# A decoder trunk on one core: x and memory read depth-first, the first block of columns computed before the rows' scales are known

## The chip, the cores and the metric

The kernel runs on one core of a Trainium2 chip. Its engines work side by side: TensorE multiplies matrices (PE in the rows; PEld is its loading of the stationary operand), VectorE (DVE) and ScalarE (ACT) work on tiles, GpSimd (POOL) does some of the same more slowly, and SyncE (SP) issues most of the transfers. The metric is the device time of one execution in microseconds (us), as a median of several runs.

## What is computed

One layer of a hybrid decoder, all in float32, with x of 1024 rows by 2048 and a memory of 256 rows by 2048:

```
h   = rmsnorm(x, norm_mix)                    # each row by 1/rms, each column by its gain
y   = h @ w_in                                # 2048 x 7184: q, k, v and gates of three mixers
mix = [stick_breaking(8 heads), gated_linear(4 heads), spatial_gating(4 groups)]
x   = x + (rmsnorm_per_head(mix) * silu(gates)) @ w_out
m   = rmsnorm(mem, norm_mem)
x   = x + cross_attention(rmsnorm(x, norm_xattn), m, w_xq, w_xkv, w_xo)
out = rmsnorm(x, final_norm)
```

The change concerns the first line, the memory's norm, and the columns of `y` that are computed first: `SB_V`, 1024 columns of v for the stick-breaking heads, and `GL_V`, 512 columns of v for the gated linear attention.

## The kernel before

Every large product is made from operands that are split in two (`hi`, a rounded copy, and `lo`, what is left), so that three matmuls stand for one: `mm3` issues hi by lo, hi by hi, lo by hi. A weight piece of 128 rows by up to 512 columns is loaded by `raw_weights` (three buffers `wr`), ScalarE casts it to `wh` and VectorE subtracts to get `wl` (three buffers each; `split_to`, L143 and L144). The left operand of all the first products is `hT`: the normed x, transposed, 2048 deep on the partitions (16 pieces `k` of 128) by 1024 rows in two halves of 512.

The order of the work is that of the program as far as the operands allow: a scheduler sorts each engine's queue ahead of time by program order and readiness. Where `pinned` is set, TensorE's instructions keep the order in which they are written. Memory pools are opened and closed by name, and a pool that is opened takes the place of one that was closed.

The stages, in order:

1. The first stage (pool `xin`). Eight row tiles of x (128 rows by 2048) and then two of memory are loaded. `normed` squares a row tile on ScalarE (L340), finds 1/rms (`rstd_of`) and scales the tile on VectorE (L348, with the gain `gbc`, which is broadcast over the partitions). `turn` transposes it on TensorE in pieces of 128 by 128 (`flip`, L180) and splits the result from PSUM into `hT`. While the next row tile is made ready, the first 256 columns of `SB_V` are computed for the tile before, from eight weight pieces that stay in memory. Then the second 256 columns are computed for all rows, with the rows in two halves. Transposed memory goes through scratch in DRAM (`memt_scr`). The results of v go to scratch (`v_scr`, L311, L312, L314).
2. Six blocks of 512 columns for all 1024 rows: the second half of `SB_V`, then `gv`, `su`, `sv`, `sg`, `gg` (`natural`, pool `st0`; each result is stored to DRAM from a tile `nt`, L460 and L461).
3. Keys and values of the memory (pool `kv`): for each of 16 `k` the transposed memory is loaded (L476) and split, two weight pieces are loaded and split, and 12 matmuls of 512 columns add into four banks `pj`, which are all that there are of that kind.
4. The rest, which the change leaves as it is: the gating unit (pool `sgu`), gated linear attention, stick-breaking attention beside the projections of k and q, the output projection, attention over the memory and the last norm.

A block's matmuls are counted in steps: in the blocks whose rows are in two halves, a step is one `k` for four row tiles, 12 matmuls; its plan is `[(k, r) for r in halves for k in range(KT)]`, 32 steps.

Of the kernel before, what the change touches and what calls it, by code (L numbers as in the profile page):

```python
# [17 lines left out]
P = 128  # L18
S = 1024
D = 2048  # L20
# [21 lines left out]
def trunk(ctx, tc, x, mem, norm_mix, w_in, w_gla_gate_up, b_gla_gate, sgu_norm, w_sgu, b_sgu,  # L42
          out_norm, w_out, norm_xattn, norm_mem, w_xq, w_xkv, w_xo, final_norm, out, dbg=None):
# [3 lines left out]
    x2d, mem2d, out2d = x[0], mem[0], out[0]  # L47
    w_in3 = w_in[0].rearrange("(k p) n -> p k n", p=P)
# [22 lines left out]
    class Operand:  # L71
        """[2048, 1024] with its first axis on partitions, as two tiles that add up to it, by four k and half."""
# [15 lines left out]
    def scratch(name, shape):  # L88
# [5 lines left out]
    make_identity(nc, ident)  # L94
# [7 lines left out]
    layout = (("out", out_norm[0], 16), ("xat", norm_xattn[0], 16), ("mem", norm_mem[0], 16), ("bg", b_gla_gate[0], 2),  # L102
              ("bs", b_sgu[0], 4))
    cols_at, n_cols = {}, 0
    for nm, _, n in layout:
        cols_at[nm] = n_cols
        n_cols += n
    cols = const.tile([P, n_cols], F32, name="cols")

    def load_cols():  # L110
        """Vectors that act per partition, one column for each 128 values."""
        rows = wraw.tile([P, 512], F32, tag="wr", name="rows")
        for nm, src, n in layout:
            c = cols_at[nm]
            sp.dma_start(rows[c:c + n, :P], src if nm == "bs" else src.rearrange("(k p) -> k p", p=P))
        tp = bank("pj")
        pe.transpose(tp[:, :n_cols], rows[:n_cols, :P], ident[:n_cols, :n_cols])
        dve.tensor_copy(cols, tp[:, :n_cols])

# [8 lines left out]
    def rstd_of(ss, n, count):  # L128
        """(ss / count + eps) ** -0.5, with a Newton step after the tables."""
# [29 lines left out]
    def weights(src, width, sub=1, hl=None, raw=None, eng=None):  # L159
        """A [P, sub * width] piece of a weight, as two tiles that add up to it."""  # L160
# [34 lines left out]
    def column_block(acts, w3, c0, evac, halves=(0, 1)):  # L195
        """[n, s] tiles of the product for 128 columns, in four groups of a load and four steps."""
# [27 lines left out]
    def weave(groups, tasks):  # L224
        """Steps in order, each task before the step that its time names, loads a group ahead."""
# [91 lines left out]
    with tc.tile_pool(name="xin", bufs=2) as xin, tc.tile_pool(name="w0", bufs=1) as w0p:  # L317
# [5 lines left out]
        def load_rows(src):  # L323
            xt = xin.tile([P, D], F32, tag="xt", name="xt", bufs=3)
            for sl in pieces:
                sp.dma_start(xt[:, sl], src[:, sl])
# [892 lines left out]
```

## Time and profile before

| | |
|---|---|
| median of 3 runs | 2186.11 us |
| lowest and highest | 2184.13 and 2188.30 us |
| the profiled execution, from its first to its last instruction | 2184.6 us |
| TensorE busy | 2125.8 us, 97% |
| VectorE busy | 1020.7 us, 47% |
| ScalarE busy | 860.9 us, 39% |
| GpSimd busy | 163.5 us, 7% |
| mean memory traffic | 106 GB/s |

The profiled execution has no time of its own beside its span; the span of 2184.6 us is set beside the median. Busy is the time in which an engine had an instruction under way. Matmuls are pipelined: a row of the trace gives a matmul's time from start to modelled end, and the distance between the starts of two matmuls in a row is what one costs in a stream.

### The profile page before, as it was taken

What the parts mean: (1) busy time and instruction counts of PE and PEld (TensorE: products, weight loads), DVE (VectorE), ACT (ScalarE), POOL (GpSimd) and SP (SyncE); (2) the same over time, 40 slices, a digit from 0 to 9 for tenths busy, and PEclk for the clock granted to TensorE, in tenths of its full rate; (3) what the DMA queues carried; (4) which work ended last, traced back from release to release, by engine and by line L of the source; (5) the groups of instructions that cost most, each with busy time, mean ns of one, the idle gap of its engine ahead of it and who ended that gap; (6) DMA issues with size and microseconds to landing.
All of it is one profiled execution on the core that took longest, in us unless ns stands there. A gap on an engine that the chain in (4) does not pass through costs nothing.

```text
span 2184.6 us, 28465 instructions
## 1 busy us (share of the span) xinstructions
PE 2125.8 (97%) x10525; PEld 1767.4 (81%) x10525; DVE 1020.7 (47%) x1984; ACT 860.9 (39%) x1987; POOL 163.5 (7%) x273
## 2 busy tenths in 40 slices
PE   6999999999999999999999999999989999999997
PEld 6998888888887767878888888888877878888885
DVE  6621211111115627375377677776753121377674
ACT  6421111221215424242356565666654121356552
POOL 2110000000000110101111111111012000000001
PEclk9999999999999999999999999999999999999999
DMA  7541321331317621313222222222267231655632
GB/s 215 151 146 49 126 87 49 97 97 49 98 55 219 184 61 44 107 34 92 78 57 55 56 63 56 61 54 56 83 192 231 69 124 49 207 201 154 216 121 92
DMA packets 181847, 231.18 MB, mean 106 GB/s; under 512 B 17270, under 2 KB 106956, under 8 KB 179532
## 3 DMA queue, kind: packets, MB, share of 16 engines
q1 hardware_dynamic: 170572, 214.68, 32.1%
q0 software_dynamic: 11136, 14.69, 2.6%
q8 instruction: 83, 1.36, 0.3%
q14 instruction: 56, 0.46, 0.1%
HBM read 177.93 MB, written 51.38 MB: 105 GB/s over the span
## 4 chain that ended last, share of the span: by engine, by line
PE 44%; DVE 8%; ACT 5%; issue 4%; DMA 2%; POOL 1%; DVEq 0%; SPq 0%; POOLq 0%; ACTq 0%
PE pj L175 31%; PE z L175 6%; PE av L175 4%; PE tr L180 1%; DVE a L865 1%; DVE a L871 1%; PE tr L175 1%; ACT a L872 1%; DMA mraw<-mix 1%; ACT t L859 1%; ACT t L860 1%; DVE t L861 1%; DVE ql L663 1%; ACT t L858 1%; DVE wl L144 1%
## 5 line engine op out<-in xcount | busy, mean ns | idle before, releaser
L144 DVE TENSOR_TENSOR wl<-wr,wh 128x512 fp32r<-128x512 f32 (+1 forms) x392 | 267.6, 683 | 773.8 <-ACT wh L143 767.6
L175 PE MATMUL pj<-slot,wh 128*128 128x512 f32 x2048 | 576.9, 398 | 1.6 <-DVE qT L144 1.6
L143 ACT CAST wh<-wr 128x512 fp32r<-128x512 f32 (+1 forms) x395 | 237.6, 602 | 798.4 <-PE av L175 548.6
L175 PE MATMUL pj<-wh,slot 128*128 128x512 f32 (+1 forms) x1760 | 500.7, 370 | 0.0
L175 PEld LDWEIGHTS pj<-slot,wh 128*128 128x128 f32 x2048 | 369.7, 188 | 72.4 <-issue 2.3
L175 PEld LDWEIGHTS pj<-wh,slot 128*128 128x128 f32 x1760 | 321.5, 190 | 54.8
L175 PE MATMUL pj<-wl,slot 128*128 128x512 f32 (+1 forms) x880 | 328.9, 374 | 1.7 <-DVE wl L144 1.5
L175 PE MATMUL pj<-slot,wl 128*128 128x512 f32 x1024 | 327.9, 391 | 0.0
L175 PEld LDWEIGHTS pj<-slot,wl 128*128 128x128 f32 x1024 | 192.2, 188 | 42.7
L175 PEld LDWEIGHTS pj<-wl,slot 128*128 128x128 f32 x880 | 167.1, 190 | 30.3 <-DVE wl L144 2.3
L175 PE MATMUL z<-wh,slot 128*128 128x512 f32 x576 | 178.6, 390 | 0.7 <-DVE slot L144 0.7
L175 PEld LDWEIGHTS z<-wh,slot 128*128 128x128 f32 x576 | 108.2, 188 | 24.1 <-DVE slot L144 1.9
L175 PE MATMUL z<-wl,slot 128*128 128x512 f32 x288 | 112.5, 391 | 4.4 <-DVE xo L982 2.7
L861 DVE SCALAR_TENSOR_TENSOR t<-z,t 128x384 f32<-128x384 f32 (+2 forms) x96 | 53.4, 556 | 94.3 <-ACT t L860 94.2
L872 ACT ACTIVATE a<-a 128x384 f32<-128x384 f32 (+2 forms) x96 | 50.4, 525 | 114.5 <-DVE a L871 114.4
L175 PE MATMUL pj<-slot,oT 128*128 128x512 f32 x384 | 92.7, 396 | 0.0
L175 PE MATMUL tr<-wh,slot 128*128 128x512 f32 x288 | 88.7, 389 | 0.0
L175 PE MATMUL av<-wh,slot 128*128 128x512 f32 x288 | 88.7, 389 | 0.0
L175 PEld LDWEIGHTS pj<-slot,oT 128*128 128x128 f32 x384 | 71.0, 188 | 15.7
L175 PE MATMUL z<-kT,qT 128*128 128x512 f32 (+3 forms) x288 | 71.1, 355 | 0.0
L175 PEld LDWEIGHTS z<-wl,slot 128*128 128x128 f32 x288 | 54.0, 188 | 17.2 <-DVE xo L982 3.6
L144 DVE TENSOR_TENSOR aTl<-tr,aTh 128x512 fp32r<-128x512 f32 (+2 forms) x112 | 55.2, 493 | 19.3 <-ACT aTh L143 18.2
(252 smaller groups left out, 2684.2 us busy)
## 6 DMA issues: line engine op xcount, KB each, us to landing
wr<-in_w_in_dram SPq DMA_DIRECT2D x216, 256.0 KB, 2.8
wr<-in_w_out_dram SPq DMA_DIRECT2D x88, 256.0 KB, 2.8
xt<-in_x_dram SPq DMA_DIRECT2D x32, 256.0 KB, 4.8
wr<-in_w_xkv_dram SPq DMA_DIRECT2D x32, 256.0 KB, 3.2
v<-v_scr POOLq DMA_DIRECT2D x64, 128.0 KB, 2.8
xr<-in_x_dram SPq DMA_DIRECT2D x32, 256.0 KB, 5.1
x<-xo SPq DMA_DIRECT2D x32, 256.0 KB, 4.4
x2t<-x SPq DMA_DIRECT2D x8, 1024.0 KB, 7.2
```

The costliest lines, as they stand in the source:

```text
L143: act.copy(hi, src)
L144: eng.tensor_tensor(out=lo, in0=src, in1=f32(hi), op=ALU.subtract)
L175: i = pe.matmul(o, l, r, start=start, stop=stop)
L180: i = pe.transpose(o, i_, ident)
L663: dve.tensor_tensor(out=gl["ql"][r_, :, hh, :].rearrange("p c (b i) -> p c b i", i=h), in0=gl["q"][r_, :].rearrange("p (c b i) -> p c b i" ...
L858: act.activation(tw, z, AF.Abs)
L859: act.activation(tw, tw, AF.Exp, scale=-1.0)
L860: act.activation(tw, tw, AF.Ln, bias=1.0)
L861: dve.scalar_tensor_tensor(out=tw, in0=z, scalar=0.0, in1=tw, op0=ALU.max, op1=ALU.add)
L865: dve.tensor_tensor_scan(out=aw[:, ::-1], data0=tw[:, ::-1], data1=tw[:, ::-1], initial=init, op0=ALU.add, op1=ALU.max)
L871: dve.tensor_tensor(out=aw, in0=z, in1=aw, op=ALU.subtract)
L872: act.activation(aw, aw, AF.Exp)
```

## The change

x and the memory are also handed over transposed (`xT`, `memT`: 2048 deep by 1024 or 256), and the gains that act per partition come as columns of one small array (`cols`, `mix`). With depth on the partitions, the gain `norm_mix` is a number per partition, while 1/rms is a number per row, that is, per column of the operand, and is known only when a whole row has been squared and summed.

- Pieces of `xT` (128 by 512) arrive one at a time. `arrive` splits a piece, times its gain, into `hT` (`split_gain`: ScalarE for hi, VectorE for lo), squares it on ScalarE and adds the square to a running sum on GpSimd.
- The block `GL_V` is computed from these unscaled operands, rows in two halves: 32 steps. Its results are scaled by 1/rms as they leave the banks; those of the first half are kept and scaled later.
- Before step 26 `scales` sums the squares over the partitions on TensorE: eight products with two columns of ones, and two with a matrix of ones, which give 1/rms in every partition (`r_all`).
- From step 27 to step 58 `rescale` loads each piece of `xT` again, multiplies it by gain and 1/rms on VectorE and splits it into the same place of `hT`. The first half of `SB_V` (512 columns wide, rows in two halves) is steps 32 to 63 and uses the rescaled operand, as does all that follows.
- The memory's pieces are loaded transposed, split with their gain, and the results are scaled by the memory's 1/rms, whose squares are taken from rows of memory loaded in the same loop (at `k` = 4 and 6).
- The transposes of x and memory, the row norms, the memory's scratch and the 256-wide passes are gone. The scratch stores of v are on SyncE. The pools of the gating unit and of the memory open after the pool `st0` closes, and the identity for later transposes is made after the first two blocks.

```diff
-        def turn_x(s, kg):
-            split_to(*hT.group(kg, s), transposes(xs[s], kg))
...
-        def turn_mem(m, kg):
-            tp = transposes(xs[ST + m], kg)
...
-            pool.dma_start(memt_scr[m][4 * kg:4 * kg + 4].rearrange("k p m -> p k m"), mt)
...
-            (pool if "at" in kw or nh == 2 else sp).dma_start(v_scr[s][:, h0:h0 + nh], vt)
+            sp.dma_start(v_scr[s][:, h0:h0 + nh], vt)
...
-    sgu_open()
     kv = Stage("kv", 2)
-    kv.open()
+    halves = (range(4), range(4, 8))
 
     with tc.tile_pool(name="st0", bufs=2) as st0:
-        natural(hT, w_in3, SB_V + 512, 512, evac_v(st0, 512, 4, tag="vt"))
...
+        with tc.tile_pool(name="xin", bufs=1) as xin:
+
+            sp.dma_start(cols, cols_in[:, :n_cols])
+            mix = xin.tile([P, KT], F32, name="mix")
+            sp.dma_start(mix, cols_in[:, n_cols:n_cols + KT])
+            squares = xin.tile([P, 2, 512], F32, name="squares")
+            r_all = xin.tile([P, 2, 512], F32, name="r_all")
+            unscaled, r_row = {}, []
+
+            def staged():
+                return xin.tile([P, 512], F32, tag="xt", name="xt", bufs=6)
+
+            def piece(k, half):
+                xt = staged()
+                sp.dma_start(xt, xT3[:, k, half * 512:half * 512 + 512])
+                return xt
+
+            def arrive(k, half):
+                xt = piece(k, half)
+                split_gain(*hT.at(k, half), xt, mix[:, k:k + 1])
+                if k == 0:
+                    act.activation(squares[:, half], xt, AF.Square)
+                else:
+                    sq = xin.tile([P, 512], F32, tag="sq", name="sq", bufs=2)
+                    act.activation(sq, xt, AF.Square)
+                    pool.tensor_tensor(out=squares[:, half], in0=squares[:, half], in1=sq, op=ALU.add)
+
+            def scales():
+                b = bank("pj")
+                for s in range(ST):
+                    mm(b[:, 2 * s:2 * s + 2], squares[:, s // 4, (s % 4) * P:(s % 4) * P + P], ones_f[:, 0:2], True, True)
+                sums_ = [bank("pj"), bank("pj")]
+                for h in range(2):
+                    mm(sums_[h], ones_f, squares[:, h], True, True)
+                for h in range(2):
+                    v_, y_, t_ = staged(), staged(), staged()
+                    dve.tensor_scalar(out=v_, in0=sums_[h], scalar1=1.0 / D, scalar2=EPS, op0=ALU.mult, op1=ALU.add)
+                    act.activation(y_, v_, AF.Ln)
+                    act.activation(y_, y_, AF.Exp, scale=-0.5)
+                    dve.scalar_tensor_tensor(out=t_, in0=y_, scalar=-0.5, in1=y_, op0=ALU.mult, op1=ALU.mult)
+                    dve.tensor_tensor(out=t_, in0=t_, in1=v_, op=ALU.mult)
+                    dve.scalar_tensor_tensor(out=r_all[:, h], in0=t_, scalar=1.5, in1=y_, op0=ALU.add, op1=ALU.mult)
+                ss = xin.tile([P, ST], F32, name="ss")
+                dve.tensor_copy(ss, b[:, 0:2 * ST:2])
+                r_row.append(rstd_of(ss, ST, D))
+                for s in range(4):
+                    act.activation(unscaled[s], unscaled[s], AF.Copy, scale=r_row[0][:, s:s + 1])
+                    sp.dma_start(nat_scr["gv"][s], unscaled[s])
+
+            def rescale(k, half):
+                xt = piece(k, half)
+                dve.scalar_tensor_tensor(out=xt, in0=xt, scalar=mix[:, k:k + 1], in1=r_all[:, half], op0=ALU.mult, op1=ALU.mult)
+                split_to(*hT.at(k, half), xt)
+
+            def keep(s, b):
+                t = unscaled[s] = xin.tile([P, 512], F32, tag=f"gv{s % 4}", name=f"gv{s}")
+                if s < 4:
+                    (dve.tensor_copy if s % 2 else act.copy)(t, b)
+                else:
+                    act.activation(t, b, AF.Copy, scale=r_row[0][:, s:s + 1])
+                    sp.dma_start(nat_scr["gv"][s], t)
+
+            by_half = [(k, r) for r in halves for k in range(KT)]
+            steps_ = row_block(hT, w_in3, GL_V, 512, keep, by_half) + \
+                row_block(hT, w_in3, SB_V, 512, evac_v(st0, 0, 4, tag="vt"), by_half)
+            extra = [[] for _ in range(64)]
+            order_ = [(k, half) for half in range(2) for k in range(KT)]
+            for n, (k, half) in enumerate(order_):
+                j = k if half == 0 else (n - 16) * 4 + 3 if n < 21 else n - 5
+                extra[j].append((arrive, k, half))
+                extra[27 + n if n < 5 else 27 + n].append((rescale, k, half))
+            extra[26].append((scales,))
+            steps_[0][0]()
+            for j, (_, do) in enumerate(steps_):
+                for f, *args in extra[j]:
+                    f(*args)
+                if j + 1 < len(steps_):
+                    steps_[j + 1][0]()
+                do[0]()
+        make_identity(nc, ident)
+        natural(hT, w_in3, SB_V + 512, 512, evac_v(st0, 512, 4, tag="vt"))
...
-        for nm, c0, func in (("gv", GL_V, AF.Copy), ("su", SG_U, AF.Gelu_apprx_tanh), ("sv", SG_V, AF.Gelu_apprx_tanh),
+        for nm, c0, func in (("su", SG_U, AF.Gelu_apprx_tanh), ("sv", SG_V, AF.Gelu_apprx_tanh),
...
+    sgu_open()
+    kv.open()
...
     for k in range(KT):
         mt = kv.tile([P, 256], F32, tag="mt", name="mt")
-        for m in range(2):
-            sp.dma_start(mt[:, m * P:m * P + P], memt_scr[m][k])
+        sp.dma_start(mt, memT3[:, k, :])
...
-        split_to(hl[0], hl[1], mt)
+        split_gain(hl[0], hl[1], mt, col("mem", k))
+        if k in (4, 6):
+            for n in range(4):
+                mr = kv.tile([P, 512], F32, tag="mr", name="mr")
+                m = k // 2 - 2
+                sp.dma_start(mr, mem2d[m * P:m * P + P, n * 512:n * 512 + 512])
+                act.activation(mr, mr, AF.Square, accum_out=ss_mem[:, m, n:n + 1])
...
-        dve.tensor_copy(vt, mem_banks[m][1])
+        dve.tensor_scalar(out=vt, in0=mem_banks[m][1], scalar1=r_mem[:, m:m + 1], scalar2=None, op0=ALU.mult)
...
-        act.copy(kt, mem_banks[m][0])
+        act.activation(kt, mem_banks[m][0], AF.Copy, scale=r_mem[:, m:m + 1])
```

## Rows read from the trace of the kernel before

**Rows 1.** The page's first part: busy time, share of the span, instructions.

```profile
PE 2125.8 (97%) x10525; PEld 1767.4 (81%) x10525; DVE 1020.7 (47%) x1984; ACT 860.9 (39%) x1987; POOL 163.5 (7%) x273
```

**Rows 2.** Windows by stage: length, busy by engine, granted clock, DMA share, GB/s.

```profile
24.43:134.42 109.99, 107.02 (x889) 104.73 (x887) 66.49 (x157) 53.33 (x152) 14.03 (x22) 1.00 0.56 161
134.42:657.31 522.89, 522.68 (x2304) 432.15 (x2303) 74.85 (x115) 92.89 (x154) 2.81 (x5) 1.00 0.27 82
657.31:706.27 48.96, 47.88 (x193) 34.45 (x192) 26.02 (x45) 26.12 (x50) 0.00 (x0) 1.00 0.72 213
```

**Rows 3.** Waits of TensorE, 0 to 250 us: total, times, longest.

```profile
PE z L180 <- DVE xt L348: 13.9, 2, 9.7
```

**Rows 4.** Timeline of TensorE: start, duration, instruction, count of merged instructions.

```profile
15.39 0.41 PE L175 MATMUL pj<-wl,slot 128*128 128x256 f32 x1
...
16.03 0.41 PE L175 MATMUL pj<-wl,slot 128*128 128x256 f32 x1
...
21.09 1.09 PE L180 MATMUL z<-ident,xt 128*128 128x128 f32 x4 [4.22 <-DVE xt L348]
...
24.43 0.60 PE L180 MATMUL z<-ident,xt 128*128 128x128 f32 x4
24.79 0.36 PE L175 MATMUL pj<-w0l,slot 128*128 128x256 f32 x1
...
119.91 0.40 PE L175 MATMUL pj<-wh,slot 128*128 128x256 f32 x2
...
120.27 0.40 PE L175 MATMUL pj<-wh,slot 128*128 128x256 f32 x2
...
601.55 0.39 PE L175 MATMUL tr<-wl,slot 128*128 128x512 f32 x1
...
602.23 0.39 PE L175 MATMUL av<-wl,slot 128*128 128x512 f32 x1
```

**Rows 5.** Groups by line and form, 0 to 150 us: count, busy, mean, idle.

```profile
L180 PE MATMUL z<-ident,xt 128*128 128x128 f32 x160 | 26.6, 295 | 17.3 <-DVE xt L348 13.9 <-DVE slot L144 3.4
```

**Rows 6.** Timeline of SyncE and ScalarE at the start; issues with median landing.

```profile
0.81 1.81 SPq L326 DMA_DIRECT2D xt<-in_x_dram  x4
...
3.96 0.60 ACT L340 ACTIVATE tr<-xt 128x512 f32<-128x512 f32 x1 [1.88 <-DMA xt<-in_x_dram]
...
5.17 0.60 ACT L340 ACTIVATE av<-xt 128x512 f32<-128x512 f32 x1 [0.48 <-DMA xt<-in_x_dram]
...
xt<-in_x_dram SPq DMA_DIRECT2D x32, 256.0 KB, 4.8
```

**Rows 7.** Timelines of GpSimd and VectorE, later stages.

```profile
720.06 1.66 POOL L543 TENSOR_TENSOR y<-y,sg 128x512 f32<-128x512 f32 x1 [570.56 <-ACT wh L143]
...
720.50 1.77 DVE L144 TENSOR_TENSOR wl<-wr,wh 128x512 fp32r<-128x512 f32 x1
...
1629.60 1.29 DVE L144 TENSOR_TENSOR slot<-mraw,slot 128x512 fp32r<-128x512 f32 x2 [2.77 <-ACT slot L143]
```

**Rows 8.** Instructions of one tile or line: ns least, median, most.

```profile
L970 POOL TENSOR_TENSOR mraw<-mraw,graw x16: 1275/1292/1645, 1617.1 to 1665.3; 128x512 f32<-128x512 f32 x16
...
L524 DVE SCALAR_TENSOR_TENSOR sv<-sv,rs_r,gn x8: 744/748/1870, 495.0 to 761.4; 128x512 f32<-128x512 f32 x8
```

**Rows 9.** Timeline of TensorE: matmuls of operands that are not split.

```profile
714.55 1.06 PE L175 MATMUL z<-sv,wT 128*128 128x128 f32 x8
...
808.10 1.12 PE L175 MATMUL z<-rr,wup 32*128 32x512 f32 x2
```

**Rows 10.** The change to the memory stage: SyncE, landing times; GpSimd's groups.

```profile
658.65 0.32 SPq L461 DMA_DIRECT2D gg<-nt  x1
...
gg<-nt SPq DMA_DIRECT2D x8, 256.0 KB, 2.0
mt<-memt SPq DMA_DIRECT2D x24, 64.0 KB, 3.1
...
L579 POOL MEMSET maskf<- 128x448 f32 x1 | 0.5, 473 | 6.4 <-DMA mix<-mt 6.4
```

More of the change, by code (lines that the diff above doesn't have):

```diff
@@ L41, in trunk @@
 @with_exitstack
-def trunk(ctx, tc, x, mem, norm_mix, w_in, w_gla_gate_up, b_gla_gate, sgu_norm, w_sgu, b_sgu,
-          out_norm, w_out, norm_xattn, norm_mem, w_xq, w_xkv, w_xo, final_norm, out, dbg=None):
+def trunk(ctx, tc, x, mem, w_in, w_gla_gate_up, sgu_norm, w_sgu, w_out, w_xq, w_xkv, w_xo, final_norm,
+          xT, memT, cols_in, out, dbg=None):
     nc = tc.nc
@@ L47, in trunk @@
     x2d, mem2d, out2d = x[0], mem[0], out[0]
+    xT3 = xT.rearrange("(k p) s -> p k s", p=P)
+    memT3 = memT.rearrange("(k p) m -> p k m", p=P)
     w_in3 = w_in[0].rearrange("(k p) n -> p k n", p=P)
@@ L100, in trunk @@
     dve.memset(eps_t, EPS)
-    layout = (("out", out_norm[0], 16), ("xat", norm_xattn[0], 16), ("mem", norm_mem[0], 16), ("bg", b_gla_gate[0], 2),
-              ("bs", b_sgu[0], 4))
+    layout = (("out", 16), ("xat", 16), ("mem", 16), ("bg", 2), ("bs", 4))
     cols_at, n_cols = {}, 0
-    for nm, _, n in layout:
+    for nm, n in layout:
         cols_at[nm] = n_cols
@@ L108, in trunk @@
     cols = const.tile([P, n_cols], F32, name="cols")
[L110 to L118, printed above, removed]
     def col(nm, k):
@@ L292, in trunk @@
     nat_scr = {nm: [scratch(f"{nm}{s}", [P, 512]) for s in range(ST)] for nm in ("su", "sv", "sg", "gv", "gg")}
-    memt_scr = [scratch(f"memt{m}", [KT, P, P]) for m in range(2)]
     kt_scr = [scratch(f"kt{m}", [P, 4, P]) for m in range(2)]
@@ L307, in f @@
         def f(s, b):
-            vt = kw["at"](s) if "at" in kw else pl.tile([P, nh, 2, P], F32, name="vt", **kw)
+            vt = pl.tile([P, nh, 2, P], F32, name="vt", **kw)
             b3 = b.rearrange("p (h d) -> p h d", d=P)
-            hi = vt[:, :, 0, :]
-            act.copy(hi.bitcast(F32R), b3)
-            dve.tensor_tensor(out=vt[:, :, 1, :].bitcast(F32R), in0=b3, in1=hi, op=ALU.subtract)
+            act.copy(vt[:, :, 0, :].bitcast(F32R), b3)
+            dve.tensor_tensor(out=vt[:, :, 1, :].bitcast(F32R), in0=b3, in1=vt[:, :, 0, :], op=ALU.subtract)
@@ L482, in trunk @@
                 mm3(mem_banks[m][n], cut(hl, m * P, m * P + P), w, k == 0, k == KT - 1)
+    r_mem = kv.tile([P, 2], F32, name="r_mem", bufs=1)
+    sst_mem = small.tile([P, 2], F32, tag="ss2", name="ss2")
+    dve.tensor_reduce(out=sst_mem, in_=ss_mem, axis=AX.X, op=ALU.add)
+    dve.tensor_copy(r_mem, rstd_of(sst_mem, 2, D))
     mem_k = []
@@ L1196, in trunk @@
         dbg(locals())
-_INS = ["x", "mem", "norm_mix", "w_in", "w_gla_gate_up", "b_gla_gate", "sgu_norm", "w_sgu", "b_sgu", "out_norm",
-        "w_out", "norm_xattn", "norm_mem", "w_xq", "w_xkv", "w_xo", "final_norm"]
+_INS = ["x", "mem", "w_in", "w_gla_gate_up", "sgu_norm", "w_sgu", "w_out", "w_xq", "w_xkv", "w_xo", "final_norm"]
 def kernel(**inputs):
@@ L1208 @@
     nc = bacc.Bacc("TRN2", target_bir_lowering=False, num_devices=1)
+    laid = {name: inputs[name] for name in _INS}
+    laid["xT"], laid["memT"] = (np.asarray(inputs[nm])[0].T for nm in ("x", "mem"))
+    laid["cols"] = np.concatenate([np.asarray(inputs[nm]).reshape(-1, P) for nm in
+                                   ("out_norm", "norm_xattn", "norm_mem", "b_gla_gate", "b_sgu", "norm_mix")]).T
     arrays, args = {}, []
-    for name in _INS:
-        a = np.ascontiguousarray(inputs[name])
+    for name in laid:
+        a = np.ascontiguousarray(laid[name])
         arrays[f"in_{name}_dram"] = a
```

88 lines of the change are left out of this document (1 added, 87 removed).

## The prediction

> **What bounds the kernel now.** The page's first part comes first: TensorE is busy for 97% of the span, VectorE for under half [rows 1]. So the question is what TensorE does and where it is idle. The windows cut at the places where its work changes [rows 2] give the answer. From 134.42 to 657.31 us, six blocks of 512 columns (the second half of v, then gv, su, sv, sg, gg) run with no gap, 522.89 / 6 = 87.15 us each. Before 134.42 lies the stage that the change rewrites. After it come the memory's keys and values, 48.96 us for 192 matmuls. At the 0.227 us of a 512-wide matmul (below) those need 43.6, so 5.4 us are lost there.
>
> What the first 134.42 us hold is read from the timeline of TensorE. Three 256-wide matmuls repeat every 0.36 us (119.91 to 120.27, [rows 4]), 0.12 us each; 768 of them are 92.2 us. Four transposes take 0.36 us (24.43 to 24.79, [rows 4]), 0.09 each; the 160 of x and memory [rows 5] are 14.4 us. The rest, 134.4 - 92.2 - 14.4 = 27.8 us, is idle time and a slow clock. TensorE first waits 9.7 us for the first scaled row and once more 4.2 us for the second, 13.9 together [rows 3]. Until 24.43 us three 256-wide matmuls take 0.64 us (15.39 to 16.03, [rows 4]), 0.213 us each: 256 columns at 1.2 GHz, the lower of the two levels. After it they run at the higher.
>
> TensorE is never long idle from there to the end, so a microsecond that the first stage gives back is a microsecond of the whole, unless a wait takes its place.
>
> **The change part by part.** I follow the time at which the memory's matmuls start, 657.31 now; the work behind it is the same.
>
> *Blocks.* The 256-wide passes become one 512-wide block. Three 512-wide matmuls repeat every 0.68 us (601.55 to 602.23, [rows 4]), 0.227 each, against 2 x 0.36 = 0.72 for the same columns. Seven blocks at 87.15 are 610.0 us. The transposes, the row of 54 vectors, the per-row norms and the memory's way through DRAM are gone.
>
> *First matmul.* Two small loads, then the first weight, then the first x piece are issued on SP. An issue costs 1.81 / 4 = 0.45 us [rows 6], so the weight is issued at 1.7 and x at 2.2. The first piece now lands 3.96 - 0.81 = 3.15 us after its issue and the next 1.2 us behind it [rows 6]. That puts the weight at 4.9, x at 6.1 and, after a 0.60 us cast, the first matmul at 6.8 us (5.9 if x does not queue behind the weight, 8.5 if it lands after 4.8 us, the median for x [rows 6]).
>
> *Slow clock.* TensorE worked without a break from 21.09 to 24.43 before it ran at the higher level [rows 4]. If dense work from 6.8 us does likewise, 3.3 us pass at 0.12 / 0.213 = 0.56 of the rate: 1.5 us lost. The other bound is all of 9.70 to 24.43, 14.7 x 0.44 = 6.5 us. I take 1.5, since the new stream has no such gaps by the budgets below.
>
> *Scales on TensorE.* Eight tiny fp32 matmuls and two of 512 columns. Eight fp32 ones of 128 columns last 1.06 us, two of 512 (32 rows high) 1.12 [rows 9], both with tails that overlap what follows: together about 1.9, with 1.06 + 2 x 1.12 = 3.3 as the upper bound if full height makes the wide ones twice as slow, and 1.1 as the lower if the tiny ones cost nothing.
>
> *The arriving operand.* One step is four row tiles, 12 x 0.227 = 2.72 us. Up to step 26, 32 x pieces and 27 weights are split on ScalarE and VectorE, and GpSimd adds 30 squares. ScalarE pays 0.6 us a pass: (27 + 2 x 32) x 0.6 = 55 us of the 73.4 that 27 steps take, so it is covered. VectorE and GpSimd are not so clear. When a GpSimd add (720.06, 1.66 us) and a VectorE subtract of two SBUF operands (720.50, 1.77 us) meet, VectorE ends at 722.27, 0.55 us after the add; alone, two such subtracts take 1.29 us, 0.61 apart [rows 7]. So VectorE stands still while GpSimd adds. The old operand was split from PSUM; the new one is split from SBUF, against those adds. As one shared resource the pair needs 27 x 0.61 (weights, [rows 7]) + 32 x 0.68 (three operands; 0.748 alone [rows 8], less the 0.07 overlap of the subtracts) + 30 x 1.29 [rows 8] = 77.0 us. TensorE needs 73.4 + 1.5 in the same steps. That is a tie, 2.1 us against us. Were they independent, VectorE's 38 us would be hidden and this term nothing. If every add is held up as the one at 720.06 was (1.65), the pair needs 87.8 and TensorE waits 14.4 - 1.5 = 12.9 us. I take 3, near the tie, for the splits run ahead by three weight buffers.
>
> The Trainium skill, GPSIMD Engine Reference, section Specifications, says that GpSimd shares its SBUF interfaces with VectorE and contends with VectorE instructions that have two SBUF inputs; the trace agrees with its 1.77 us, and it speaks against this part of the change.
>
> *Rescale in place.* After the scales the chain is: two reductions read, logarithm, exponential, a Newton step (about 4.2 us for the first half, from three VectorE passes of 0.75 [rows 8] behind two ScalarE passes of 0.6 and one read of 0.7), then the x piece again (4.8 to land), and 0.75, 0.60 and 1.29 - 0.61 = 0.68 to scale and split it: 11.0 us. The first rescaled piece is wanted at step 32, six steps or 16.3 us later. It fits with 5.3 us spare, and ScalarE can split the weights of steps 27 to 31 in the gaps. After that each step wants 0.61 + 0.68 + 0.61 = 1.9 us of VectorE in 2.72. If that cover goes, step 32 is late, and everything behind it. I allow 1 us (0 to 5), and 1 us (0 to 3) for the v stores, which now stand on SP's queue between the weights and the x pieces.
>
> *DMA.* Weights and x are read twice in these 64 steps, 512 KB in 2.72 us or 193 GB/s. The memory stage now moves 213 [rows 2], so it is hidden; without that cover each step would lose the difference.
>
> *Memory stage.* One load of memory in place of two per step, but eight more loads and 4.8 us of ScalarE for its squares. Between all of the 5.4 lost us won and as many lost again, I take zero.
>
> Sum: 6.8 + 610.0 + 1.5 + 1.9 + 3 + 1 + 1 = 625.2, against 657.31: 32.1 us won. The profiled execution spans 2184.6 us and the median of the runs is 2186.11, 1.5 more. 2184.6 - 32.1 + 1.5 = 2154.0 us.
>
> **Rivals.** *A, the memory stage starts late.* The pools of the gating unit and of the memory now open after the pool of the 512-wide results closes. At a later change of pools GpSimd's first write into the new pool waited 6.4 us for the last store of the old one [rows 10]. If the memory's loads wait so, the last store (issued 658.65, 2.0 to land) ends at 660.7; two loads of the gating unit go first (0.8), then 3.1 to land and 0.8 to split [rows 10]: 665.4. TensorE idles 8.1 us and pays the slow clock's 1.5 again: 2163.6. For it: every bank of the first kind is taken by the memory's own sums, so nothing can fill the gap. Against: the memory's tiles may lie where only the first stage's were, and then load early, as now.
>
> *B, VectorE and GpSimd bind the first block.* The 12.9 us from above in place of 3: 2163.9, and up to 2168 if the scales are late by as much as they have spare.
>
> *C, slower than before: the clock stays low.* If waits between steps keep TensorE at the lower level, 512 columns cost 0.427 in place of 0.227, over the first block's 32 steps 32 x 12 x 0.2 = 77 us. It decides from 32.1 / 77 = 42% of the block, 13 steps, on; with all of it the time is 2154 + 77 = 2231, with 60% of it 2200. For it: before, the level was low through the whole start with its 4.2 us gap. Against: the granted clock was full in all three windows from 24.43 on [rows 2], and gaps by the budget are tenths of a microsecond a step.
> The Trainium skill, TensorE: Matmul & The Clock Gate, section Loop structure matters more than you think, warns of loops in which TensorE waits for a load between matmuls and then runs at the lower rate; the first 24 us agree (0.213 us for 256 columns).
>
> **How the numbers follow.** Forecast 0.58 (its own range 2146 to 2160: no stalls and a better memory stage at one end, the bounds of the smaller terms at the other), A 0.18, B 0.16, C 0.05, and 0.03 for waits that eat the gain just about. The range 2146 to 2168 leaves out C, the last case and the edges of the others, 2 in 10. Faster by over 0.2% (about the spread of the runs before, 2184.13 to 2188.30, and what a measurement can tell) 0.93, within it 0.02, slower 0.05.
>
> **What would show it.** First matmul near 6.8 us and full clock by about 11; twelve 512-wide matmuls per 2.72 us in the first block with waits on VectorE of 3 us in all (B: 13); adds of about 1.3 us with VectorE's splits stretched to 1.8 beside them; no wait of TensorE at the first rescaled piece; the memory's first matmul at about 625 us right behind the last gg matmul (A: 8 us of idle time there). The prediction is wrong if TensorE waits at the scales or at the pool change for more than a few microseconds, or if the sum of the stage before 134.42 us does not shrink to about 102 us (625.2 less six blocks).

## The result and the profile after

The changed kernel takes 2166.45 us (median of four runs, 2165.18 to 2167.51) against 2187.2 (2184.13 to 2190.08) on the same chip: a ratio of 0.9906, interval 0.9894 to 0.9918. It is faster, as forecast, by 20.7 us, where 32 were worked out. The time lies near the upper end of the range of 2146 to 2168, where rival B was put, and outside the forecast's own 2146 to 2160. The profiled execution spans 2164.6 us, 20.0 less than before.

The page's first part, which answers to [rows 1]:

```profile
PE 2108.2 (97%) x10000; PEld 1735.2 (80%) x10000; DVE 1077.2 (50%) x1978; ACT 890.6 (41%) x1975; POOL 186.3 (9%) x271
```

Windows of the changed kernel, in the columns of [rows 2]; the third is the memory stage:

```profile
6.35:49.90 43.55, 37.92 (x138) 29.17 (x139) 42.09 (x33) 33.78 (x59) 33.07 (x21) 0.92 0.69 221
49.90:100.00 50.10, 46.09 (x200) 36.95 (x199) 29.92 (x36) 21.43 (x39) 15.13 (x10) 0.97 0.42 122
640.22:691.09 50.87, 47.41 (x194) 35.02 (x193) 28.32 (x51) 28.80 (x54) 0.67 (x1) 1.00 0.79 246
```

VectorE, under half busy over the whole, is busy for 42.09 of the 43.55 us in which the operand arrives, with GpSimd at 33.07 beside it. TensorE does not fill that stretch, and its granted clock is not full. (The column of the granted clock has no record of the start, until the level first rises near 11 us; there the level is read from the distance of the matmuls.) The waits of TensorE in the first 300 us, where [rows 3] had 13.9 us:

```profile
PE pj L166 <- DVE wl L135: 9.6, 6, 2.1
PE pj L166 <- ACT slot L138: 6.3, 1, 6.3
PE z L166 <- DVE wl L135: 0.6, 1, 0.6
```

The 6.3 is the start. The other 10.2 us are waits for VectorE's split of a weight: 9.6 while the operand arrives, the last at 61.32 us, and 0.6 that ends at 187.4 us, in the second block, where the kernels without adds on GpSimd wait too (1.0 us in kernels 1 and 2 below). The timeline of TensorE shows where they fall and what follows:

```profile
6.35 0.80 PE L166 MATMUL pj<-wl,slot 128*128 128x512 f32 x1 [6.35 <-ACT slot L138]
...
11.38 0.39 PE L166 MATMUL pj<-wl,slot 128*128 128x512 f32 x1
...
24.62 0.74 PE L166 MATMUL pj<-wl,slot 128*128 128x512 f32 x1 [2.09 <-DVE wl L135]
25.16 1.05 PE L166 MATMUL pj<-wh,slot 128*128 128x512 f32 x2
...
28.37 0.39 PE L166 MATMUL pj<-wl,slot 128*128 128x512 f32 x1
...
35.69 0.50 PE L166 MATMUL pj<-wl,slot 128*128 128x512 f32 x1 [1.02 <-DVE wl L135]
...
40.77 0.50 PE L166 MATMUL pj<-wl,slot 128*128 128x512 f32 x1 [2.06 <-DVE wl L135]
...
61.32 0.50 PE L166 MATMUL pj<-wl,slot 128*128 128x512 f32 x1 [2.04 <-DVE wl L135]
...
65.77 0.39 PE L166 MATMUL pj<-wl,slot 128*128 128x512 f32 x1
...
95.74 1.84 PE L166 MATMUL pj<-ones_f,squares 128*128 128x2 f32 x16
97.44 1.96 PE L166 MATMUL pj<-squares,ones_f 128*128 128x512 f32 x4
98.84 0.79 PE L166 MATMUL z<-wl,slot 128*128 128x512 f32 x1
...
640.22 0.39 PE L166 MATMUL pj<-wl,mh 128*128 128x512 f32 x1
```

From 6.35 to 11.38 us run 12 matmuls: 5.03 us in place of 2.72, the lower level, 2.3 us lost. After the wait of 2.09 us the level falls again: from 24.62 to 28.37 nine matmuls take 3.75 us in place of 2.04. The same follows the waits that end at 40.77 and 61.32 us (twelve matmuls in 4.45 us from 61.32 to 65.77), not those that end at 35.69 or 56.26: 5.1 us in all. The scales take 95.74 to 98.84, 3.1 us (each fp32 matmul stands as two records).

Why the weight is late is read from VectorE and GpSimd (timelines, merged):

```profile
35.56 3.48 DVE L139 SCALAR_TENSOR_TENSOR slot<-xt,mix,slot 128x512 fp32r<-128x512 f32 x2
38.96 1.75 DVE L135 TENSOR_TENSOR wl<-wr,wh 128x512 fp32r<-128x512 f32 x1
40.64 3.46 DVE L139 SCALAR_TENSOR_TENSOR slot<-xt,mix,slot 128x512 fp32r<-128x512 f32 x2
44.02 1.76 DVE L135 TENSOR_TENSOR wl<-wr,wh 128x512 fp32r<-128x512 f32 x1
```

```profile
31.77 13.46 POOL L370 TENSOR_TENSOR squares<-squares,sq 128x512 f32<-128x512 f32 x8
```

The additions as one group, 0 to 130 us (busy and mean ns behind the bar):

```profile
L370 POOL TENSOR_TENSOR squares<-squares,sq 128x512 f32<-128x512 f32 x30 | 48.2, 1611 | 21.4 <-ACT sq L369 20.1
```

From 31.77 us on GpSimd adds without a pause, eight in 13.46 us (1611 ns on average over all thirty), and each VectorE split meets an add: about 1.7 us apiece, where [rows 7] have 0.61 for one alone. VectorE's queue holds two x pieces for each weight, so in such a stretch one weight comes per 5.06 us (38.96 to 44.02), while TensorE uses one in 2.72. ScalarE does not hold the splits up: from 10 to 72 us it waits 0.4 us for GpSimd to free a buffer of squares, and VectorE waits 0.3 us for ScalarE. All 32 x pieces are split by 70 us; after that VectorE idles, with the scales not wanted for a while.

How many us the changed kernel is ahead at the same work of both:

| place | ahead |
|---|---|
| memory's first matmul (657.31; 640.22) | 17.1 |
| behind the memory stage (706.27; 691.09) | 15.2 |
| behind the gated attention (1073.75; 1061.28) | 12.5 |
| end of the stick-breaking attention (1595.67; 1580.76) | 14.9 |
| last matmul (2170.18; 2152.58) | 17.6 |
| end | 20.0 |

### The profile page after: what moved, and what is told of

It reads as the page before. It is cut to its first block, busy times and chain, and to the rows that moved or that the text cites. A ratio compares the mean times of both kernels' runs of the same rounds, so it can differ in the third digit from the quotient of the medians.

```text
span 2164.6 us, 27461 instructions
## 1 busy us (share of the span) xinstructions
PE 2108.2 (97%) x10000; PEld 1735.2 (80%) x10000; DVE 1077.2 (50%) x1978; ACT 890.6 (41%) x1975; POOL 186.3 (9%) x271
## 4 chain that ended last, share of the span: by engine, by line
PE 43%; DVE 9%; ACT 5%; issue 5%; DMA 2%; POOL 1%; SPq 0%; DVEq 0%; POOLq 0%; ACTq 0%
PE pj L166 31%; PE z L166 6%; PE av L166 4%; DVE a L839 1%; PE tr L171 1%; DVE a L845 1%; ACT t L833 1%; ACT t L834 1%; PE tr L166 1%; DVE t L835 1%; ACT a L846 1%; DMA mraw<-mix 1%; DVE ql L637 1%; ACT t L832 1%; DVE wl L135 1%
## 5 line engine op out<-in xcount | busy, mean ns | idle before, releaser
L135 DVE TENSOR_TENSOR wl<-wr,wh 128x512 fp32r<-128x512 f32 x408 | 297.4, 730 | 715.8 <-ACT wh L134 707.8
L134 ACT CAST wh<-wr 128x512 fp32r<-128x512 f32 x408 | 252.2, 618 | 747.6 <-PE av L166 518.8
L166 PE MATMUL pj<-wh,slot 128*128 128x512 f32 x1536 | 478.6, 393 | 0.0
L166 PEld LDWEIGHTS pj<-wh,slot 128*128 128x128 f32 x1536 | 291.8, 190 | 60.6 <-DVE slot L139 0.3
L166 PE MATMUL pj<-wl,slot 128*128 128x512 f32 x768 | 304.2, 396 | 17.3 <-DVE wl L135 10.7
L166 PE MATMUL z<-wh,slot 128*128 128x512 f32 x640 | 197.9, 390 | 0.1
L166 PEld LDWEIGHTS pj<-wl,slot 128*128 128x128 f32 x768 | 145.8, 190 | 51.6 <-DVE wl L135 15.1
L166 PEld LDWEIGHTS z<-wh,slot 128*128 128x128 f32 x640 | 120.2, 188 | 25.8 <-DVE slot L135 0.9
L166 PE MATMUL z<-wl,slot 128*128 128x512 f32 x320 | 125.6, 392 | 4.8 <-DVE xo L956 3.5
L166 PEld LDWEIGHTS tr<-wh,slot 128*128 128x128 f32 x320 | 60.1, 188 | 12.4
```

Of the source, the lines that this page charges most:

```text
L134: act.copy(hi, src)
L135: eng.tensor_tensor(out=lo, in0=src, in1=f32(hi), op=ALU.subtract)
L166: i = pe.matmul(o, l, r, start=start, stop=stop)
```

## The experiments

Times of different kernels are compared by their ratio to the kernel before, run on the same chip.

**1. The adds on VectorE.**

```
-                    pool.tensor_tensor(out=squares[:, half], in0=squares[:, half], in1=sq, op=ALU.add)
+                    dve.tensor_tensor(out=squares[:, half], in0=squares[:, half], in1=sq, op=ALU.add)
```

> Theory L (VectorE's splits of two SBUF operands stand still while GpSimd adds the squares, so that the pair needs about 2.2 us for a split and an add together): with the adds on VectorE itself, 0.69 us each in place of 1.60 beside it, VectorE needs 27 x 0.61 + 32 x 0.68 + 30 x 0.69 = 59 us in the 73.4 us of the first 27 steps, TensorE's waits on VectorE's weight split in the first 65 us fall from 9.6 us to under 2, the clock stays at the higher level from about 11 us on, the memory's first matmul comes at 625 to 628 us in place of 640.2, and the time is about 2152 us (13 to 15 below the changed kernel). Rival (the x loads or ScalarE are late, or the order in which the pieces arrive): the waits stay, and the time is within 2 us of the changed kernel's 2166, or above it, since VectorE has 30 operations more.

Measured: 2148.99 us, ratio 0.9835 (0.9816 to 0.9854); the memory's first matmul at 624.55. TensorE's waits in the first 300 us behind the start, and its first window:

```profile
...
PE z L166 <- DVE wl L135: 1.0, 1, 1.0
PE pj L166 <- DVE vt L301: 0.3, 1, 0.3
PE pj L166 <- DVE wl L135: 0.2, 1, 0.2
...
```

```profile
6.35:49.90 43.55, 43.55 (x183) 35.76 (x184) 42.97 (x68) 41.53 (x74) 0.00 (x0) 1.00 0.88 284
```

VectorE does 68 operations in the stretch in which it did 33. TensorE has no gap, and its level does not fall again once it has risen; its first twelve matmuls, from 6.25 to 11.23 us, run at the lower level here too. One word in one line gives 15.7 us at the memory's first matmul. The x loads and ScalarE were not late: the same loads run at 284 GB/s here.

**2. No adds at all.**

```
-                if k == 0:
-                    act.activation(squares[:, half], xt, AF.Square)
-                else:
-                    sq = xin.tile([P, 512], F32, tag="sq", name="sq", bufs=2)
-                    act.activation(sq, xt, AF.Square)
-                    pool.tensor_tensor(out=squares[:, half], in0=squares[:, half], in1=sq, op=ALU.add)
+                act.activation(squares[:, half], xt, AF.Square)
```

> Left out: the sum of the squares over the depth; each piece's squares overwrite the one before, so the scales come from the last 128 rows alone (times 16). No addition is made by any engine, all else stays. Theory L: waits of TensorE on VectorE in the first 65 us under 1 us, full clock from about 11 us, the memory's first matmul near 625 us, time about 2152 us, as with the adds on VectorE. Rival (loads or ScalarE late): no change, about 2166 us.

Two divisors, not shown, are changed along with it, so that the scales keep their size. Measured: 2150.42 us (one run), the memory's first matmul at 624.27. With the adds on VectorE it stands at 624.55, so there they cost next to nothing.

**3. The adds on GpSimd, the arrivals in the program's order.**

```
-                split_gain(*hT.at(k, half), xt, mix[:, k:k + 1])
+                hi, lo = hT.at(k, half)
+                g = mix[:, k:k + 1]
+                tc.keep_in_program_order(act.activation(hi, xt, AF.Copy, scale=g))
+                tc.keep_in_program_order(dve.scalar_tensor_tensor(out=lo, in0=xt, scalar=g, in1=f32(hi), op0=ALU.mult, op1=ALU.subtract))
...
-                    act.activation(sq, xt, AF.Square)
+                    tc.keep_in_program_order(act.activation(sq, xt, AF.Square))
```

> The splits and squares of the arriving x pieces are held to the program's order, so that x no longer runs two pieces ahead for each weight; the adds stay on GpSimd. If the pair's capacity is the cause (theory L: 27 x 0.6 + 2 x 0.7 + 30 x 2.24 = 84.8 us in 73.4 of TensorE), about 8 to 11 us of waits remain, spread over steps up to the 27th, and the time is within 4 us of 2166. If it is the run-ahead alone that puts the pair's work too early, the waits go to under 2 us, and the time falls by about 10 us to 2156.

Measured: 2153.95 us, ratio 0.9852 (0.9836 to 0.9868); the memory's first matmul at 626.67, waits on weight splits 2.2 us. This is the rival's outcome, but for 0.2 us of waits, and it corrects my theory. VectorE and GpSimd in this kernel:

```profile
40.90 0.68 DVE L135 TENSOR_TENSOR wl<-wr,wh 128x512 fp32r<-128x512 f32 x1
41.50 1.78 DVE L367 SCALAR_TENSOR_TENSOR slot<-xt,mix,slot 128x512 fp32r<-128x512 f32 x1
43.20 0.68 DVE L135 TENSOR_TENSOR wl<-wr,wh 128x512 fp32r<-128x512 f32 x1
43.81 1.77 DVE L367 SCALAR_TENSOR_TENSOR slot<-xt,mix,slot 128x512 fp32r<-128x512 f32 x1
45.50 0.68 DVE L135 TENSOR_TENSOR wl<-wr,wh 128x512 fp32r<-128x512 f32 x1
```

```profile
40.99 1.74 POOL L373 TENSOR_TENSOR squares<-squares,sq 128x512 f32<-128x512 f32 x1 [0.57 <-ACT sq L372]
43.70 1.32 POOL L373 TENSOR_TENSOR squares<-squares,sq 128x512 f32<-128x512 f32 x1 [0.98 <-ACT sq L372]
```

The hold-up is still there: each x split beside an add takes 1.77 us. But with one x piece for each weight there is one add per step, the weight's split (0.68) falls into GpSimd's pause, and a step needs 2.45 us of VectorE in 2.72. So neither cause is enough alone. GpSimd's hold-up costs the time when two x pieces and two adds stand between two weights; in the program's order 2.1 us of the 15.7 are left. In kernel 1 two x pieces and two adds still stand between two weights in VectorE's queue, and with the adds on VectorE that order costs no wait.

**4. Each add done twice on GpSimd.**

```
+            again = xin.tile([P, 2, 512], F32, name="again")
...
                     pool.tensor_tensor(out=squares[:, half], in0=squares[:, half], in1=sq, op=ALU.add)
+                    pool.tensor_tensor(out=again[:, half], in0=squares[:, half], in1=sq, op=ALU.add)
```

> Each of GpSimd's 30 additions is made a second time into a tile that nothing reads. Theory L: the pair of GpSimd and VectorE gets 30 x 1.5 = 45 us more work, of which little is covered: the waits in the first stage grow by 35 to 45 us, with more of the lower clock, and the time is 2200 to 2215 us. Rival (GpSimd works beside VectorE without holding it up): GpSimd needs 30 x 2 x 1.6 = 96 us at the most and the scales come some 20 us later, which the rescaled pieces mostly have to spare; under 10 us more than 2166.

Measured: 2194.83 us (one run; 2185.45 for the kernel before on that chip), slower than before the change; the memory's first matmul at 669.88, 29.7 later than with one add. Waits of TensorE in the first 300 us, two windows, and the largest wait of ScalarE from 10 to 108 us:

```profile
PE pj L166 <- DVE wl L135: 23.2, 12, 3.4
...
PE z L166 <- DVE wl L135: 4.9, 3, 3.4
```

```profile
6.35:49.90 43.55, 33.04 (x108) 23.98 (x108) 34.84 (x25) 23.41 (x40) 38.71 (x25) 0.88 0.55 180
49.90:100.00 50.10, 34.60 (x102) 24.97 (x103) 29.36 (x26) 24.53 (x42) 47.82 (x32) 0.76 0.34 104
```

```profile
ACT sq L370 <- POOL again L372: 45.5, 27, 2.1
```

The size was less than I said, about 30 us of time by the ratios against 34 to 49. Nor does this run confirm the hold-up of VectorE, for a second path opens in it. The squares have two buffers (`sq`), and ScalarE waits 45.5 us for GpSimd to free one (0.4 us in the changed kernel); the casts of the weights stand behind these squares in its queue, and VectorE idles for 28.6 us from 10 to 108 us, waiting for ScalarE. The run shows that TensorE loses when GpSimd is slower still, and not by which of the two paths. What shows the hold-up are the single operations, 0.68 us alone and 1.75 to 1.78 beside an add, and kernels 1 to 3.

The Trainium skill, Trainium Architecture — The Big Picture, section What this means for kernel authors, calls the port that VectorE and GpSimd share an exclusive lock and not a split of bandwidth. The traces agree: 0.68 us of a split alone, 1.78 beside one add, and in kernel 3 that split ends 0.55 us behind the add (41.50 + 1.78 against 40.99 + 1.74), about its own length, so it waited the add out.

**5 to 7. Warm-up and the memory stage, first try.** All with the adds on VectorE. Kernel 5 puts small matmuls ahead of the first real one, kernel 6 holds the gating unit's first loads to their place, kernel 7 does both and moves the load of the column vectors (`cols`) behind step 4.

```
+        warm = bank("av")
+        for _ in range(44):
+            mm(warm[:, :P], ones_r, ones_r, True, True)
```

```
-            sp.dma_start(t[nm], nat_scr[nm][s])
+            i = sp.dma_start(t[nm], nat_scr[nm][s])
+            if s < 2:
+                tc.keep_in_program_order(i)
```

> The adds on VectorE, and 44 matmuls of 128 columns on a tile of ones (into a bank that nothing reads) ahead of the first real matmul. In the kernel with the adds on VectorE the first twelve real matmuls run from 6.25 to 11.2 us at the lower level, which costs 2.3 us against 2.72 us a dozen. If the level rises because TensorE has been at work, the first real matmuls take 0.227 us apiece, the first matmul stays at 6.3 us, the memory's first matmul comes at 622.3 in place of 624.55 us, and the time is 2146 to 2147.5. Rival (the level rises at a set time after the start, or the ones matmuls delay the first real one): no gain, 2149, or up to 1 us above it.

> The adds on VectorE, and the first two rows' loads of sv, su and sg for the gating unit (six of 256 KB) held to their place in the program, behind the memory's loads. If those loads are what slows the memory stage (they move 1.5 MB in it, and ScalarE waits 13 to 16 us there for the memory's weights), it falls from 50.65 us to 49 or less (before: 48.96), and the time by 1 to 2 us to 2147 to 2148. Rival (the late casts and stores at the stage's start set it, or the bytes do not matter): the stage stays at 50 to 51, the time at 2149, and more if the gating unit then waits for its rows.

> The adds on VectorE, the matmuls on ones, the held loads, and the load of the column vectors moved from the front of SP's queue to behind the fourth step (0.45 us of issue ahead of the first weight). If the parts add up: first real matmul at 5.8 us, the memory's first matmul near 621.9, its stage 49 us, and the time 2144.5 to 2147. If the held loads or the ones do nothing, 2147 to 2149.

Measured: 5: 2155.66, ratio 0.9856 (0.9840 to 0.9871); 6: 2149.11, 0.9824 (0.9809 to 0.9838); 7: 2156.46, 0.9860 (0.9844 to 0.9877). Kernel 5 failed by its own size:

```profile
1.51 9.65 PE L166 MATMUL av<-ones_r 128*128 128x128 f32 x44 [1.51 <-DVE ones_r L99]
10.96 0.73 PE L166 MATMUL pj<-wl,slot 128*128 128x512 f32 x1
11.49 1.05 PE L166 MATMUL pj<-wh,slot 128*128 128x512 f32 x2
```

The 128-column matmuls, each with its own weight load, started every 0.213 us, not every 0.107 as I reckoned from the 0.213 us of 256 columns, so the first real one came 4.7 us late (the memory stage then took 52.98 us besides). And after 9.4 us of them TensorE was still at the lower level (two matmuls in 0.86). In kernel 6 the memory stage took 50.52 us against 50.65 in kernel 1: the gating unit's bytes do not slow it, and its two large stalls stay (1.6 and 1.7 us; 1.9 and 1.6 in kernel 1). In kernel 7 the stage took 50.37 us, so the held loads did not give the 49 us hoped for there either.

**8 to 10. Warm-up with wide matmuls; the norm's and the mixing weight's loads later.** With the adds on VectorE again; kernel 8 has ten matmuls of 512 columns, kernel 9 loads `gn` and `wn` at the memory's step 10, kernel 10 does both.

```
+        warm = bank("av")
+        for _ in range(10):
+            mm(warm.rearrange("p (a n) -> p a n", a=4), ones_r, ones_r.unsqueeze(1).to_broadcast([P, 4, P]), True, True)
```

```
-        sp.dma_start(gn, sgu_norm.to_broadcast([P, 512]))
-        sp.dma_start(wn, w_sgu[0].rearrange("g t s -> t g s"))
...
+        if k == 10:
+            sgu_load_consts()
```

> The adds on VectorE, and ten matmuls of 512 columns on the tile of ones ahead of the first real one (the 44 of 128 columns took 0.22 us each, until 10.96 us, twice what was planned, and the level was still the lower one behind them, so they tested nothing but a late start). At 0.427 us each these end near 5.8 us, before the first operand is ready. If dense 512-column work raises the level, the first real matmul stays near 6.3 us and the dozen behind it takes 2.7 us in place of 5.0: the memory's first matmul at 622.3 in place of 624.55, time about 2147. Rival (the level rises at a set time after the start whatever TensorE does): 624.5 and 2149.

> The adds on VectorE, and the loads of gn and wn (256 KB each, landing in 4.4 and 4.8 us) held back to the memory stage's step 10 instead of standing between its first weights. With the gating unit's loads held back the stage kept its two stalls near its steps 3 and 5 (1.6 and 1.5 us), so those bytes were not the cause. If gn and wn are, the first stall goes, the stage takes 48.5 to 49.2 us in place of 50.65, and the time is 2147 to 2148. Rival (the weights' casts, late behind the eight evacuations of gg and the table load of ScalarE at the stage's start): the stage stays at 50.5 and the time at 2149.

> Both of these together. If both hold, the memory's first matmul at 622.3, its stage 49, and the time 2144 to 2146, the fastest of all; if neither, 2149.

Measured: 8: 2151.46, ratio 0.9838 (0.9824 to 0.9853); 9: 2150.54, 0.9834 (0.9819 to 0.9850); 10: 2150.74, 0.9836 (0.9821 to 0.9850). None differs from kernel 1's 0.9835 by more than the intervals. In kernel 8 the level was up when the first operand came, and the memory's first matmul stood at 622.42, as expected:

```profile
6.39 0.52 PE L166 MATMUL pj<-wl,slot 128*128 128x512 f32 x1 [0.24 <-ACT slot L138]
...
7.90 0.39 PE L166 MATMUL pj<-wl,slot 128*128 128x512 f32 x1
8.13 0.62 PE L166 MATMUL pj<-wh,slot 128*128 128x512 f32 x2
```

The 2.1 us were lost again behind it, 1.5 of them in the memory stage (52.11 us). In kernel 9 the first large stall of the memory stage went from 1.9 us to 0.1, but the next weight lost 0.8 and the stage took 51.78 us: the time was lost later in the stage instead. In kernel 10 the memory's first matmul stood at 623.55 us and its stage took 52.08. This suggested that something binds the stage on average.

**11 and 12. Five buffers for the memory's weights,** with the adds on VectorE; 12 has kernel 8's ten matmuls too.

```
-            w = weights(w_xkv3[:, k, n * 512:n * 512 + 512], 512)
+            kr = kv.tile([P, 512], F32, tag="kr", name="kr", bufs=5)
+            sp.dma_start(kr, w_xkv3[:, k, n * 512:n * 512 + 512])
+            w = weights(None, 512, raw=kr)
```

> The adds on VectorE, and the memory's weights land in five buffers of their own in place of the three that all weights share. Holding back loads moved the stage's first stall but not its sum (50.5 and 51.8 us against 50.65). Theory: the stage is bound by the round trip of three buffers: 3.1 us from issue to landing, 0.62 of cast, 0.69 of subtract, with hand-overs some 4.7 us in all, and 4.7 / 3 = 1.57 us a weight against TensorE's 1.36; 32 weights are 50 us. With five, 0.94 us a weight, the stage falls to 45 to 47 us (43.6 are TensorE's own), and the time by 3 to 5 us to 2144 to 2146. Rival (the DMA's rate, 248 GB/s in this stage, or ScalarE's late casts): it stays at 49 to 51.

> The same with the ten matmuls of 512 columns on ones ahead, which brought the memory's first matmul to 622.4 us in place of 624.55 and yet left the time at 2151, since the stages behind lost 4 us. If those losses belong to the memory stage's stalls, they go with them: 2142 to 2145. If they come from the order in which the later stages are scheduled, which the ten matmuls shift, this kernel ends 1 to 3 us behind the one without them, although its memory stage starts 2 us earlier.

Measured: 11: 2144.22, ratio 0.9808 (0.9795 to 0.9822), the lowest of all, though the intervals of kernels 1 and 6 still overlap with its own; 12: 2147.17, 0.9825 (0.9811 to 0.9838). The memory stage of kernels 1, 6 and 11, and the landing of kernel 11's weights:

```profile
624.55:675.20 50.65, 46.55 (x193) 35.36 (x192) 28.48 (x51) 28.96 (x54) 0.67 (x1) 1.00 0.78 248
623.90:674.42 50.52, 46.93 (x193) 35.15 (x192) 26.89 (x46) 27.65 (x50) 0.67 (x1) 1.00 0.73 221
626.08:671.72 45.64, 45.05 (x193) 35.91 (x192) 29.28 (x51) 29.43 (x55) 0.67 (x1) 1.00 0.76 251
```

```profile
kr<-in_w_xkv_dram SPq DMA_DIRECT2D x26, 256.0 KB, 4.2
```

45.64 us against 50.65. Fourteen of kernel 11's sixteen steps take 2.80 us, so 44.8 us are TensorE's own here. The theory fits: with three buffers a weight is issued when VectorE has read a buffer (in kernel 1 a split ends at 636.64 us and the next load is issued at 636.67), and that chain (3.2 us to land there, cast, split) is shared by three. The DMA's mean rate, 251 GB/s against 248, would not by itself exclude a limit of the DMA, since kernel 11 moves 11.5 MB in its shorter stage and kernel 1 12.6 in its own; kernel 6 speaks against it, with 11.2 MB in 50.52 us, at 221 GB/s. Two things stay open. Kernel 11 also loads two more weights ahead of the stage (26 of the 32 are issued in it, 28 in kernel 1), and no run tells this head start from the round trip. And three buffers do not bind throughout: in kernel 1 the last eleven weights lose 0.15 us together.

Kernel 12 starts the memory stage 1.4 us earlier than 11 and ends 2.2 later in the trace. It loses 0.9 in the memory stage (46.54 us) and 2.1 at one place, the end of the stick-breaking attention. First kernel 11's row there and its window behind it, then kernel 12's:

```profile
1552.21 0.39 PE L166 MATMUL av<-aTl,v 128*128 128x256 f32 x1 [1.35 <-ACT sq L890]
...
1553.40:1556.00 2.60, 2.60 (x14) 2.15 (x13) 2.05 (x5) 1.64 (x5) 0.29 (x1) 1.00 0.35 101
```

```profile
1552.59 0.39 PE L166 MATMUL av<-aTl,v 128*128 128x256 f32 x1 [1.89 <-ACT sq L893]
...
1553.40:1556.00 2.60, 2.60 (x11) 2.11 (x10) 2.30 (x5) 1.59 (x4) 0.29 (x1) 0.54 0.44 102
```

After 1.89 us of waiting the granted clock is 0.54, after 1.35 it stays at 1.00. So the second reading held in the main, and most of the loss is the clock: in the shifted order one wait was 0.5 us longer, and the level fell behind it. That the 0.5 us decided it is not shown, for elsewhere the level fell behind one of two equal waits (last section).

## Why the prediction was right or wrong

Its sum for the memory's first matmul, term by term:

| term | predicted | measured |
|---|---|---|
| first matmul | 6.8 | 6.35 |
| seven blocks | 610.0 | 12 matmuls per 2.72 as before: 610.0 |
| slow clock at the start | 1.5 | 2.3 |
| scales on TensorE | 1.9, at most 3.3 | 3.1 |
| VectorE and GpSimd | 3, at most 12.9 | 9.6 of waits, 5.1 of lower level |
| step 32 late, v stores | 1 + 1 | no wait at step 32; the rest of the sum, 3.8, is not told apart (0.6 of it is the wait that ends at 187.4 us) |
| sum | 625.2 | 640.2 |

**The step that failed** is "I take 3, near the tie, for the splits run ahead by three weight buffers". The tie was struck between totals, 77.0 us of work in 74.9. The totals were fair: in order, the same work leaves TensorE almost no wait (kernel 3). What they hid is the order. The queue did not run ahead by weights but by x pieces, two to a weight, with two adds, so all the pair's work came in the first 70 us, and VectorE idled later. The bound from above, every add held up, was what happened in that time: the adds took 1.6 us on average against the 1.65 of the bound. So rival B was the mechanism. It was worked out at 12.9 us of waits and gave 9.6, and it had no term for the level that falls behind such waits (5.1 us). By the prediction's own sign the forecast was wrong: the stage ahead of the six blocks took 117.3 us (640.22 less 522.9), not about 102.

**Luck.** That the time lies in the range, 2.6 us from B's 2163.9, is partly luck. The memory's first matmul came 5.1 us later than B's terms put it (635.1), the memory stage lost 1.9 us more, and then 7.5 us were won in places that the prediction does not name.

**What held.** The start came as forecast, to half a microsecond (its bound of 8.5 us does not add up, since 2.2 + 4.8 + 0.6 are 7.6, but nothing hangs on it). The blocks came as forecast. TensorE did not wait at the first rescaled piece. The memory's first matmul came right behind the last of gg, so rival A is out: the memory's first pieces and its rows were loaded long before, from 163.2 us on. Rival C in the form that I gave it, the level low from step to step, did not come; but its cause did, in three places of nine matmuls each, and three is what I should have priced.

**Scales and slow clock** were mis-sized only. The scales took 3.1 us, near the bound of 3.3, but not by its terms: the tiny matmuls took 1.70 us where 1.06 was the price, the two wide ones 1.40 where the bound had 2.24. The slow clock at the start took 2.3 us in place of 1.5.

**Memory stage.** "I take zero" between 5.4 won and lost; 1.9 were lost. Kernel 11 points to the round trip of three buffers, in which the changed stage has other loads too (`gn`, `wn`, six tiles of the gating unit): holding these back one kind at a time did not help, and two more buffers gave 5 us. That the same bound made the 5.4 us of before is likely, as its weights had three buffers as well, but no run was made of it; and about 1.2 of the 5.4 are no stall, since a step without one takes 2.80 us in this stage and not 2.72.

**Behind it** I counted no change; there the kernel first lost 2.7 us and then won 7.5. Two losses of 1.45 us are the clock, at equal waits; this is told below. Of the gain, 2.4 us are the end of the stick-breaking attention, where TensorE waits 1.99 us before the change with the clock falling to 0.66, and 1.61 after it with none. 1.1 us are a wait for the queries, 1.6 us before and 0.5 after. 1.8 us come from the last product (by `w_xo`), whose matmuls start every 0.233 us before and every 0.227 after at full clock in both; and 2.4 us lie behind the last matmul, or rather behind VectorE's last operation, which ends 6.5 us after that matmul's start in both kernels; the sum is 7.7, and shifts of both signs, of up to 1.1 us each, make it 7.5. Why these last two changed is open; no run was made for them.

With the adds on VectorE the memory's first matmul is at 624.55 us, close to the 625.2 of the sum: the path that the forecast had, no stalls in the arrival, is that of a kernel one line away from this one. The agreement of the number is partly luck. There too the scales (3.1) and the slow clock (2.3) took 2.0 us more than their prices, and the 3 us were priced for adds on GpSimd, which that kernel does not have.

## What to carry to other kernels

Before giving GpSimd an elementwise pass "for free", list the VectorE instructions with two SBUF operands that run beside it, in the order of the queue and not as totals, and ask which of them TensorE waits for next. Where a stage loses time at no fixed place, and removing one stall moves the loss, count the buffers in its round trip. And price a wait of TensorE of 2 us at up to twice its length, since the clock may fall behind it.

## What the runs showed of the hardware

The same wait lowers the clock in one kernel and not in another. In the gated attention TensorE waits for VectorE's `d`, before the change (first row) as after it (second row):

```profile
858.82 2.02 PE L175 MATMUL z<-ql,d 128*128 128x128 f32 x16 [2.54 <-DVE d L666]
```

```profile
843.41 3.30 PE L166 MATMUL z<-ql,d 128*128 128x128 f32 x16 [2.52 <-DVE d L640]
```

The wait is 2.54 and 2.52 us; the sixteen matmuls behind it take 2.02 us at full clock and 3.30 at 0.58. The next such wait, 2.53 and 2.54 us, goes the same way. In kernel 11 the first of the two is followed by 0.55 and the second by 1.00. What decides it is left open. The Trainium skill, TensorE: Matmul & The Clock Gate, section Loop structure matters more than you think, warns of long waits for loads between matmuls. Here waits of 1.9 to 2.5 us, for VectorE or ScalarE, were enough in some places. So a kernel with such waits can differ by some 1.5 to 2 us a place when something ahead of them shifts, which is as much as several of these experiments set out to win.

Also unexpected: 9.4 us of 128-column matmuls left TensorE at the lower level (kernel 5), and behind ten of 512 columns in 4.6 us it was at the higher (kernel 8).
